# Keys and values of the memory tokens made feature-major, from memory given feature-major as well

## The chip, the cores and the metric

The kernel runs on one core of a Trainium2 chip. The metric is the device time of one launch in microseconds (us), lower is better. Three runs of the kernel before gave a median of 2762.11 us (2761.31 to 2764.7).

## The reference

One layer of a streaming encoder with 512 tokens of width 2048, in fp32: a token mixer of four parts, cross-attention of 4 heads into 256 memory tokens, and a SwiGLU network. Only the cross-attention touches the change:

```
def memory_cross_attention(h, m, wq, wkv, wo):      # m = rmsnorm(mem, g[MEM_NORM]), 256 x 2048
    q = (h @ wq).reshape(bsz, T, XA_HEADS, XA_HEAD_DIM)
    k, v = jnp.split(m @ wkv, 2, axis=-1)           # 4 heads of 512 columns each
    s = jnp.einsum('bthd,bmhd->bhtm', q, k) * XA_HEAD_DIM ** -0.5
    p = jax.nn.softmax(s, axis=-1)
    o = jnp.einsum('bhtm,bmhd->bthd', p, v).reshape(bsz, T, D_MODEL)
    return o @ wo
```

The norm of a memory token is one factor for its row (from the mean square of its 2048 values) and a gain per feature, which the kernel multiplies into the weights.

## The kernel before, in words

Every fp32 operand of a matrix product is split into a high and a low part (hi by a rounding copy on ScalarE, the engine ACT; lo by a subtraction on VectorE, the engine DVE). A product is three matmuls: hi by hi, hi by lo, lo by hi (`mul3`, L177 to L179). Weights arrive as `raw` tiles of 256 rows by 512 columns (512 KB, issued on the SyncE queue, SP), and L161 and L162 make `whi` and `wlo` of them, in two halves of 128 x 512, with the gain as a factor. Each of `raw`, `whi` and `wlo` has three buffers. PSUM has five accumulators `mm` and three tiles `ps` for transposes and small products.

The program begins with **the key stage**, from 0 to about 113 us. `k_proj` runs `kv_proj` for four heads. The memory (256 x 2048) is loaded with tokens on the partitions in eight pieces `memt`; 32 transposes on the matrix engine (L265) make it feature-major, and it is split into the tiles called `act`. For a head, `proj_b` makes eight chunks of 256 features: memory stationary, weights moving, for each of two token tiles and two feature tiles three matmuls of 512 columns. That is 96 matmuls a head, into two `mm` accumulators with tokens on the partitions. ACT evicts each with the token's factor `rmem` (L290), eight transposes (L293) make the head feature-major, the result is split into `kh` and `kl`, and both go to DRAM. `finish` computes `rmem` from the loaded rows, and the feature-major memory is written to DRAM (`m_d`) for later.

Then `x_startup` loads the 512 token rows as four tiles `xt` of 1 MB, normalises them and transposes them (L231, 64 transposes) for the first projection out of x (`z`). Its code stands behind the key stage, but the order of instructions on each engine is made by a scheduler over the whole program, so that loads and norms of x, and the first weights of z, stand among the last instructions of the key stage.

**The value stage** (about 715 to 832 us) reads `m_d` back (`v_load`) and runs the same `kv_proj` for four value heads, while the last mixer (`ssd`, marked as high priority) puts its own small products, and much DVE work, between them. Later `value_out` multiplies the values by the output weights `xa_wo`, evicts with an ACT copy, and writes `vw_d`.

## Time and profile before

| | before |
|---|---|
| median of three runs | 2762.11 us |
| the profiled execution | 2761.12 us |
| its span in the trace | 2759.1 us |
| around the span | 2.0 us |
| PE (matmuls) busy | 2673.8 us, 97% |
| DVE, ACT busy | 1942.6 us (70%), 1266.6 us (46%) |
| granted TensorE clock, mean | 0.99 |
| memory traffic | 428.08 MB, mean 155 GB/s |

PE does matmuls, PEld is its weight load, which overlaps. The span is the time from the first to the last recorded instruction. The page cuts the span in stretches and names, for each instruction, what ended the wait before it.

### The profile page before, as it was taken

Reading aid. Unit: us, or ns where it says so; the run is one execution under the profiler, and the core shown is the slowest. Engines: PE = TensorE matmul, PEld = TensorE weight load, DVE = VectorE, ACT = ScalarE, POOL = GpSimd, SP = SyncE. Lnnn points to the kernel's source line nnn. Section 1 sums busy time; section 2 is a strip of 40 time slices with the busy share of each in tenths; the row PEclk is TensorE's granted clock in tenths of the full one; section 3 lists DMA queues with packets and bytes.
Section 4 is the critical chain, followed back from the end, with each engine's and each line's share of the span. In section 5 each row is a group of like instructions: output and inputs, shape, how many; then the busy total and the mean of one; then the engine's idle time right before and its main releaser. Section 6 shows DMA issues by size and latency. Waiting matters only on the chain.

```text
span 2759.1 us, 35296 instructions
## 1 busy us (share of the span) xinstructions
PE 2673.8 (97%) x13426; PEld 2246.2 (81%) x13426; DVE 1942.6 (70%) x2866; ACT 1266.6 (46%) x1927; POOL 148.9 (5%) x225
## 2 busy tenths in 40 slices
PE   8999999999999999999978999999999998999997
PEld 6788788878788877888867888888888887888885
DVE  5735557446662255434589989898989898999985
ACT  5623423233552245423455454454445455655552
POOL 0000000100000001000000000000000000000004
PEclk9999999999999999999989999999999999999998
DMA  8632322343676358532553443333334336577765
GB/s 292 238 102 86 96 69 81 107 130 115 222 241 232 98 171 308 186 106 85 197 207 131 148 121 121 126 117 124 121 120 123 118 115 225 202 193 189 183 172 186
DMA packets 159283, 428.08 MB, mean 155 GB/s; under 512 B 18173, under 2 KB 30346, under 8 KB 148234
## 3 DMA queue, kind: packets, MB, share of 16 engines
q1 hardware_dynamic: 140682, 355.57, 39.7%
q0 software_dynamic: 18432, 70.27, 8.8%
q8 instruction: 105, 1.72, 0.3%
q14 instruction: 64, 0.52, 0.1%
HBM read 351.30 MB, written 74.47 MB: 154 GB/s over the span
## 4 chain that ended last, share of the span: by engine, by line
PE 83%; DVE 8%; DMA 5%; ACT 2%; issue 2%; SPq 0%; POOL 0%; DVEq 0%; ACTq 0%; POOLq 0%
PE mm L178 17%; PE mm L179 17%; PE mm L177 17%; PE mm L1088 11%; PE ps L1088 8%; PE mm L1091 6%; PE ps L1091 4%; DVE wlo L162 1%; DMA raw<-in_xa_wkv_dram 1%; DVE wlo L992 1%; PE ps L533 1%; PE ps L537 1%; DMA vw_d<-at_e 1%; DMA raw<-in_w_gu_dram 1%; DVE L L992 1%
## 5 line engine op out<-in xcount | busy, mean ns | idle before, releaser
L162 DVE SCALAR_TENSOR_TENSOR wlo<-raw,PA,whi 128x512 fp32r<-128x512 f32 x368 | 263.4, 748 | 300.4 <-ACT whi L161 300.0
L161 ACT ACTIVATE whi<-raw,PA 128x512 fp32r<-128x512 f32 x368 | 248.5, 720 | 399.5 <-PE mm L178 213.3
L1088 PE MATMUL mm<-L,whi 128*128 128x512 f32 x1448 | 367.7, 396 | 15.7 <-ACT f_x L1111 8.6
L177 PE MATMUL mm<-act,whi 128*128 128x512 f32 x832 | 330.3, 397 | 0.0
L179 PE MATMUL mm<-act,wlo 128*128 128x512 f32 x832 | 327.4, 394 | 0.0
L178 PE MATMUL mm<-act,whi 128*128 128x512 f32 x832 | 326.9, 393 | 0.0
L1088 PEld LDWEIGHTS mm<-L,whi 128*128 128x128 f32 x1448 | 263.5, 191 | 64.7 <-ACT f_x L1111 9.6
L991 ACT CAST whi<-raw 128x1024 fp32r<-128x1024 f32 x176 | 185.1, 1052 | 237.4 <-PE mm L1088 71.2
L1088 PE MATMUL ps<-L,whi 128*128 128x512 f32 x1016 | 254.8, 392 | 0.0
L177 PE MATMUL mm<-whi,act 128*128 128x512 f32 x640 | 251.9, 394 | 2.9 <-ACT act L158 2.5
L178 PE MATMUL mm<-wlo,act 128*128 128x512 f32 x640 | 251.1, 393 | 1.8 <-DVE wlo L162 1.8
L179 PE MATMUL mm<-whi,act 128*128 128x512 f32 x640 | 250.2, 392 | 0.2 <-DVE act L159 0.2
L159 DVE TENSOR_TENSOR wlo<-raw,whi 128x1024 fp32r<-128x1024 f32 x92 | 112.4, 1225 | 192.2 <-ACT whi L158 192.0
L177 PE MATMUL mm<-whB,B 128*128 128x512 f32 x592 | 231.1, 392 | 7.7 <-ACT whB L991 7.7
L178 PE MATMUL mm<-wlB,B 128*128 128x512 f32 x592 | 231.3, 391 | 1.3 <-DVE wlB L992 1.3
L179 PE MATMUL mm<-whB,B 128*128 128x512 f32 x592 | 231.0, 390 | 0.0
L992 DVE TENSOR_TENSOR wlo<-raw,whi 128x1024 fp32r<-128x1024 f32 x176 | 214.3, 1219 | 5.2 <-ACT whi L991 5.2
L1091 PEld LDWEIGHTS mm<-L,wlo 128*128 128x128 f32 x1448 | 198.0, 191 | 18.1 <-DVE wlo L992 4.0
L1088 PEld LDWEIGHTS ps<-L,whi 128*128 128x128 f32 x1016 | 182.7, 189 | 32.6
L1091 PE MATMUL mm<-L,wlo 128*128 128x256 f32 x1448 | 203.2, 283 | 2.8 <-DVE wlo L992 2.8
L991 ACT CAST whi<-sum 128x1024 fp32r<-128x1024 f32 x132 | 138.0, 1048 | 128.8 <-DVE wlo L992 64.6
L992 DVE TENSOR_TENSOR wlo<-sum,whi 128x1024 fp32r<-128x1024 f32 x132 | 161.7, 1225 | 43.3 <-ACT whi L991 42.5
(443 smaller groups left out, 4628.8 us busy)
## 6 DMA issues: line engine op xcount, KB each, us to landing
raw<-in_w_gu_dram SPq DMA_DIRECT2D x186, 512.0 KB, 3.5
raw<-in_w_in_dram SPq DMA_DIRECT2D x88, 512.0 KB, 3.7
rawB<-in_w_down_dram SPq DMA_DIRECT2D x40, 1024.0 KB, 5.5
raw<-in_xa_wkv_dram SPq DMA_DIRECT2D x64, 512.0 KB, 4.5
raw<-in_w_out_dram SPq DMA_DIRECT2D x32, 512.0 KB, 3.9
raw<-in_xa_wo_dram SPq DMA_DIRECT2D x32, 512.0 KB, 6.0
raw<-in_xa_wq_dram SPq DMA_DIRECT2D x32, 512.0 KB, 3.9
raw<-vw_d SPq DMA_DIRECT2D x28, 512.0 KB, 4.4
```

The source lines that it names most:

```text
L159: nc.vector.tensor_tensor(lo, src, hi.bitcast(F32), op=ALU.subtract)
L161: nc.scalar.activation(hi, src, AF.Copy, scale=scale)
L162: nc.vector.scalar_tensor_tensor(lo, src, scale, hi.bitcast(F32), op0=ALU.mult, op1=ALU.subtract)
L177: nc.tensor.matmul(o, ah, bh, start=start, stop=False, skip_group_check=reopen)
L178: nc.tensor.matmul(o, ah, bl, start=False, stop=False, skip_group_check=reopen)
L179: nc.tensor.matmul(o, al, bh, start=False, stop=stop, skip_group_check=reopen)
L533: nc.tensor.matmul(h64(tp)[:, h], A[:, h], Xe[:, h], start=True, stop=True)
L537: nc.tensor.matmul(h64(tp)[:, h], Pm[:, h], half(Y, s, 1)[:, h], start=True, stop=True)
L991: nc.scalar.copy(hl[0], src)
L992: nc.vector.tensor_tensor(hl[1], src, hl[0].bitcast(F32), op=ALU.subtract)
L1088: nc.tensor.matmul(bank, wh[:, k], t[k].rearrange("p s n -> p (s n)"), start=k == 0 and m in (1, 2, 5), stop=k == 7, **kw)
L1091: nc.tensor.matmul(bank[:, 0:256], wl[:, k], t[k][:, 0], start=False, stop=k == 7, **kw)
```

## The change

A second copy of the memory, transposed on the host, is an input: `mem_t`, four blocks of 128 features x 4 x 256 tokens. Each block is loaded (512 KB) and split with its high and low part side by side in one tile. In `kv_proj` the weights become the stationary operand and the memory the moving one: for each pair of feature tile and output tile one matmul of 512 columns (`wh` by hi and lo together) and one of 256 columns (`wl` by hi). The results are feature-major at once, in four `mm` accumulators a head; ACT copies the 256 columns that hold `wh` by lo out of PSUM, and DVE adds the other 256 to them. The 32 transposes of the memory and the eight of each head are gone.

The token factors now lie along the free axis. For the keys `rmem` is written to DRAM (`r_d`, 1 KB) and read back broadcast to all partitions as `R` (`k_r`), and DVE multiplies each key tile by it. The rows with tokens on the partitions are still loaded (`memr`, two tiles of 1 MB, in the chunks 5 and 7 of the first head) for the norm alone. For the values the factor moves to `value_out`, whose eviction becomes an ACT activation with a scale.

```
-    def mem_lhs(mt):
-        return lambda k, t: tuple(m[:, k % 8, t * P:(t + 1) * P] for m in mt[k // 8])
+    def mem_tiles():
+        return [ap_.tile([P, 4, 2, MEM], F32R, name="act") for _ in range(4)]
     def kv_proj(mt, c0, dst, pl, pre=None, done=None):
-        def evict(t, o):
-            kt = pl.tile([P, 512], F32, name="k_t", bufs=2)
-            nc.scalar.activation(kt, o, AF.Copy, scale=rmem[:, t:t + 1])
-            tp = ps.tile([P, 4, P], F32, name="ps")
+        o = [mm.tile([P, 512], F32, name="mm") for _ in range(4)]
+        for kc in range(KT // 2):
+            wh, wl = weights(xa_wkv, kc * 2 * P, c0, 4)
+            if pre:
+                pre(kc)
             for j in range(4):
-                nc.tensor.transpose(tp[:, j], kt[:, j * P:(j + 1) * P], ident)
-            split(hi[:, :, t * P:(t + 1) * P], lo[:, :, t * P:(t + 1) * P], tp)
-        proj_b(mem_lhs(mt), KT, xa_wkv, 0, c0, evict, range(MT_), 4, pre=pre, done=done)
+                js = slice(j * P, (j + 1) * P)
+                for k in (2 * kc, 2 * kc + 1):
+                    nc.tensor.matmul(o[j], wh[:, k % 2, js], mt[k // 4][:, k % 4].rearrange("p s m -> p (s m)"),
+                                     start=k == 0, stop=k == KT - 1, **kw)
+                for k in (2 * kc, 2 * kc + 1):
+                    nc.tensor.matmul(o[j][:, 0:MEM], wl[:, k % 2, js], mt[k // 4][:, k % 4, 0], start=False,
+                                     stop=k == KT - 1, **kw)
+        kt = []
+        for j in range(4):
+            kt.append(pl.tile([P, MEM], F32, name="k_t", bufs=4))
+            nc.scalar.copy(kt[j], o[j][:, MEM:])
+            nc.vector.tensor_tensor(kt[j], o[j][:, 0:MEM], kt[j], op=ALU.add)
+        R = done() if done else None
+        for j in range(4):
+            if R is not None:
+                nc.vector.tensor_tensor(kt[j], kt[j], R, op=ALU.mult)
+            split(hi[:, j], lo[:, j], kt[j])
...
+        def factors():
+            ss = sm.tile([P, MT_], F32, name="nr_s2")
+            for t in range(MT_):
+                sumsq(rows[t], ss[:, t:t + 1], pl)
+            mean_rsqrt(rmem, ss, MT_, D)
+            nc.sync.dma_start(r_d.rearrange("t p -> p t"), rmem)
+            nc.sync.dma_start(R, r_d.rearrange("t p -> (t p)").partition_broadcast(P))
+            for q in range(4):
+                nc.gpsimd.dma_start(m_d[q], mt[q].rearrange("p a s b -> p (a s b)").bitcast(F32))
+            return R
...
         for c in range(4):
             def evict(t, o):
                 e = pl.tile([P, 512], F32, name="at_e", bufs=2)
-                nc.scalar.copy(e, o)
+                nc.scalar.activation(e, o, AF.Copy, scale=rmem[:, t:t + 1])
```

The scheduler gives the engines new orders in the key stage, at the passage to z and in the value stage; elsewhere only the eviction of `value_out` has another operation. Three places follow. In a row stand the line, the operation, what it writes and what it reads; numbers tell buffers apart. Lines of the changed kernel are one higher in the helpers (`split` is L160 and L163 there) and eleven higher behind `k_proj`.

First, DVE at the passage from the first to the second key head. Before (`wlo_456` to `wlo_496` are the second head's weights, `kl_130` the first head's keys):

```order
L162 SCALAR_TENSOR_TENSOR wlo_456<-raw_453,PA_84,whi_455 128x512 x2
L159 TENSOR_TENSOR kl_130<-ps_401,kh_129 128x4x128
L139 COPY PB_85<-ps_425 128x93
L162 SCALAR_TENSOR_TENSOR wlo_476<-raw_473,PA_84,whi_475 128x512
L159 TENSOR_TENSOR kl_130<-ps_410,kh_129 128x4x128
L140 TENSOR_SCALAR PH_86<-PB_85 128x88
L162 SCALAR_TENSOR_TENSOR wlo_476<-raw_473,PA_84,whi_475 128x512
L162 SCALAR_TENSOR_TENSOR wlo_496<-raw_493,PA_84,whi_495 128x512 x2
```

After (`wlo_465` is the third weight tile of the second head, `k_r` is `R`):

```order
L163 SCALAR_TENSOR_TENSOR wlo_465<-raw_462,PA_84,whi_464 128x512
L286 TENSOR_TENSOR k_t_347<-k_t_347,k_r_128 128x256
L286 TENSOR_TENSOR k_t_350<-k_t_350,k_r_128 128x256
L286 TENSOR_TENSOR k_t_353<-k_t_353,k_r_128 128x256
L160 TENSOR_TENSOR kl_130<-k_t_347,kh_129 128x256
L160 TENSOR_TENSOR kl_130<-k_t_350,kh_129 128x256
L160 TENSOR_TENSOR kl_130<-k_t_353,kh_129 128x256
L286 TENSOR_TENSOR k_t_356<-k_t_356,k_r_128 128x256
L163 SCALAR_TENSOR_TENSOR wlo_465<-raw_462,PA_84,whi_464 128x512
L163 SCALAR_TENSOR_TENSOR wlo_489<-raw_486,PA_84,whi_488 128x512
```

The multiplications by `R` and three of the four low parts now stand between the two halves of one weight tile of the second head.

Second, DVE at the passage from the keys to z. Before (`wlo_1231`, `wlo_1263` and `wlo_1295` are the first weights of z, `act_1021` the transposed x):

```order
L318 TENSOR_SCALAR xt_1091<-xt_1091,nr_r_1096 128x2048
L162 SCALAR_TENSOR_TENSOR wlo_1231<-raw_1228,PA_84,whi_1230 128x512 x2
L162 SCALAR_TENSOR_TENSOR wlo_1263<-raw_1260,PA_84,whi_1262 128x512 x2
L159 TENSOR_TENSOR kl_798<-ps_963,kh_797 128x4x128
L162 SCALAR_TENSOR_TENSOR wlo_1295<-raw_1292,PA_84,whi_1294 128x512
L159 TENSOR_TENSOR kl_798<-ps_972,kh_797 128x4x128
L159 TENSOR_TENSOR act_1021<-ps_1112,act_1020 128x4x128
```

After (`wlo_1330` is the first weight tile of z, `kl_857` the last head's keys, the names with `1195` to `1198` the norm of the fourth x tile, whose load is the last of four). The five rows ahead of this piece are the scaling of the third x tile, the last two additions of the head and two of its low parts:

```order
L286 TENSOR_TENSOR k_t_1060<-k_t_1060,k_r_128 128x256
L286 TENSOR_TENSOR k_t_1063<-k_t_1063,k_r_128 128x256
L238 TENSOR_SCALAR mr_v_1196<-nr_s_1192 128x1
L160 TENSOR_TENSOR act_1120<-ps_1211,act_1119 128x4x128
L160 TENSOR_TENSOR kl_857<-k_t_1060,kh_856 128x256
L160 TENSOR_TENSOR kl_857<-k_t_1063,kh_856 128x256
L149 TENSOR_SCALAR nr_r_1195<-mr_v_1196 128x1
L160 TENSOR_TENSOR act_1120<-ps_1218,act_1119 128x4x128
L150 TENSOR_SCALAR nr_r_1195<-nr_r_1195 128x1
L160 TENSOR_TENSOR act_1120<-ps_1225,act_1119 128x4x128
L152 TENSOR_TENSOR rsq_t_1198<-nr_r_1195 128x1
L163 SCALAR_TENSOR_TENSOR wlo_1330<-raw_1327,PA_84,whi_1329 128x512
```

The first low weights of z stood ahead of the last keys and of the transposed x, and now stand behind both and behind the scaling of three x tiles. On the SP queue the loads of x at this passage stood so before (`raw` out of `xa_wkv` are weights of the keys, out of `w_in` those of z; the first x tile is four rows ahead of this piece):

```order
L316 DMA xt_1049<-in_x_dram 128x2048
L166 DMA raw_841<-in_xa_wkv_dram 128x2x512
L166 DMA raw_861<-in_xa_wkv_dram 128x2x512
L166 DMA raw_881<-in_xa_wkv_dram 128x2x512
L316 DMA xt_1070<-in_x_dram 128x2048
L316 DMA xt_1091<-in_x_dram 128x2048
L166 DMA raw_901<-in_xa_wkv_dram 128x2x512
L166 DMA raw_921<-in_xa_wkv_dram 128x2x512
L166 DMA raw_941<-in_xa_wkv_dram 128x2x512
```

And after, with all four x tiles:

```order
L327 DMA xt_1127<-in_x_dram 128x2048
L167 DMA raw_982<-in_xa_wkv_dram 128x2x512
L167 DMA raw_1006<-in_xa_wkv_dram 128x2x512
L167 DMA raw_1030<-in_xa_wkv_dram 128x2x512
L327 DMA xt_1148<-in_x_dram 128x2048
L327 DMA xt_1169<-in_x_dram 128x2048
L327 DMA xt_1190<-in_x_dram 128x2048
L167 DMA raw_1327<-in_w_in_dram 128x2x512
L167 DMA raw_1359<-in_w_in_dram 128x2x512
```

The last three weight tiles of the keys stood behind the x tiles; now three x tiles stand back to back behind these weights, straight ahead of z's.

Third, DVE at the passage from the first to the second value head. Before (`wlo_6312` is a weight tile, the names with `sd` belong to the mixer that runs between):

```order
L682 TENSOR_TENSOR sd_L_5919<-ps_5943,sd_L_5919 128x512
L162 SCALAR_TENSOR_TENSOR act_5735<-ps_5906,PB_85,act_5734 128x128
L682 TENSOR_TENSOR sd_L_5919<-ps_5943,sd_L_5919 128x512
L162 SCALAR_TENSOR_TENSOR wlo_6312<-raw_6309,PA_84,whi_6311 128x512
L695 TENSOR_TENSOR sd_t_5966<-ps_5963,sa_eG_1676 128x512
L688 TENSOR_TENSOR sd_y_5961<-ps_5952,sd_Xd_5939 128x512
L709 TENSOR_TENSOR sd_h_5972<-ps_5969,sd_h_5972 128x512
L697 TENSOR_TENSOR sd_y_5961<-sd_y_5961,sd_t_5966 128x512
L162 SCALAR_TENSOR_TENSOR wlo_6312<-raw_6309,PA_84,whi_6311 128x512
```

After (`wlo_6453` is the second weight tile of the second value head, `kl_6201` the first head's values; its fourth addition and first low part stand just ahead of this piece):

```order
L160 TENSOR_TENSOR kl_6201<-k_t_6401,kh_6200 128x256
L708 TENSOR_TENSOR sd_y_6060<-sd_y_6060,sd_t_6065 128x512
L720 TENSOR_TENSOR sd_h_6071<-ps_6068,sd_h_6071 128x512
L725 TENSOR_TENSOR sd_y_6060<-sd_y_6060,sd_z_6074 128x512
L669 TENSOR_TENSOR sd_L_6112<-sd_L_6112,C_83 128x1024
L733 TENSOR_SCALAR sd_vv_6082<-sd_ss_6077 128x2
L160 TENSOR_TENSOR kl_6201<-k_t_6404,kh_6200 128x256
L149 TENSOR_SCALAR sd_rr_6084<-sd_vv_6082 128x2
L160 TENSOR_TENSOR kl_6201<-k_t_6407,kh_6200 128x256
L150 TENSOR_SCALAR sd_rr_6084<-sd_rr_6084 128x2
L163 SCALAR_TENSOR_TENSOR wlo_6453<-raw_6450,PA_84,whi_6452 128x512
```

The evictions of the value heads stood far behind this piece before; the last addition and the four low parts of the first head now stand ahead of the second half of `wlo_6453`.

59 lines of the change are left out of this document (22 added, 37 removed).

## The prediction

> **What bounds the kernel now.** I read the page's first part, its chain that ended last, and then the two stretches that the change rewrites.
>
> ```profile
> PE 2673.8 (97%) x13426; PEld 2246.2 (81%) x13426; DVE 1942.6 (70%) x2866; ACT 1266.6 (46%) x1927; POOL 148.9 (5%) x225
> PE 83%; DVE 8%; DMA 5%; ACT 2%; issue 2%; SPq 0%; POOL 0%; DVEq 0%; ACTq 0%; POOLq 0%
> ```
>
> PE bounds it nearly everywhere, so a matmul removed counts in full, and so does each microsecond in which PE waits. The idle time sits in few places. The windows of the key stage, of the passage to z and of the first value heads (columns: PE, PEld, DVE, ACT, POOL busy, granted clock, DMA share, GB/s):
>
> ```profile
> 30.00:40.00 10.00, 7.79 (x38) 5.77 (x36) 5.98 (x17) 4.87 (x8) 1.07 (x2) 1.00 0.84 301
> 40.00:50.00 10.00, 10.00 (x48) 8.19 (x47) 5.72 (x10) 5.05 (x9) 1.07 (x2) 1.00 1.03 334
> 80.00:90.00 10.00, 8.79 (x43) 6.99 (x42) 7.85 (x27) 7.35 (x12) 0.00 (x0) 1.00 0.92 325
> 100.00:110.00 10.00, 9.25 (x40) 7.07 (x39) 9.13 (x21) 6.54 (x12) 0.00 (x0) 1.00 0.64 203
> 110.00:120.00 10.00, 9.11 (x60) 7.09 (x60) 8.74 (x15) 8.32 (x16) 1.07 (x2) 1.00 0.80 258
> 720.00:780.00 60.00, 55.98 (x289) 46.26 (x288) 52.96 (x125) 33.85 (x79) 0.00 (x0) 1.00 0.60 200
> ```
>
> PE loses 2.2 us in 30 to 40, 1.2 in 80 to 90, 0.75 and 0.89 around the passage to z. The DMA engines are at 0.84 to 1.03 in the key stage, and DVE is at 53 of 60 us among the value heads: the two resources that the change loads more.
>
> **Fewer transposes.** PE's timeline, around four memory transposes:
>
> ```profile
> 30.34 0.39 PE L179 MATMUL mm<-whi,act 128*128 128x512 f32 x1
> 30.57 0.60 PE L265 MATMUL ps<-C,memt 128*128 128x128 f32 x4
> 30.92 0.48 PE L177 MATMUL mm<-whi,act 128*128 128x512 f32 x1
> 31.23 0.40 PE L178 MATMUL mm<-wlo,act 128*128 128x512 f32 x1
> ...
> 32.16 0.40 PE L179 MATMUL mm<-whi,act 128*128 128x512 f32 x1
> 34.59 0.50 PE L177 MATMUL mm<-whi,act 128*128 128x512 f32 x1 [2.03 <-ACT act L158]
> ```
>
> The plain pace of the key heads is in PE's rows of the last head, five steps in 1.13 us, 0.226 each:
>
> ```profile
> 109.16 0.39 PE L177 MATMUL mm<-whi,act 128*128 128x512 f32 x1
> ...
> 110.29 0.39 PE L179 MATMUL mm<-whi,act 128*128 128x512 f32 x1
> ```
>
> Start to start, L179 to L178 is 0.89 us with four transposes between, of which the two matmuls take 0.23 each: 0.44 for four, 0.11 each. 32 of memory, 32 of keys and 32 of values go: 96 x 0.11 = **-10.7 us**.
>
> **Another mix of matmuls.** A head had 96 of 512 columns; it gets 64 of 512 and 64 of 256, two and two. Such pairs run elsewhere in this kernel:
>
> ```profile
> 1996.94 1.11 PE L1091 MATMUL mm<-L,wlo 128*128 128x256 f32 x8
> 1997.89 2.00 PE L1088 MATMUL ps<-L,whi 128*128 128x512 f32 x8
> 1999.73 1.12 PE L1091 MATMUL ps<-L,wlo 128*128 128x256 f32 x8
> ```
>
> Eight narrow ones take 0.95 us to the next start, 0.119 each; eight wide ones 1.84, 0.230. A head becomes 64 x (0.230 + 0.119) = 22.3 us against 96 x 0.226 to 0.228 = 21.8. Eight heads: **+4.4 us** (3.5 to 5).
>
> ```profile
> L1091 PEld LDWEIGHTS mm<-L,wlo 128*128 128x128 f32 x1448 | 198.0, 191 | 18.1 <-DVE wlo L992 4.0
> ```
>
> In that pattern a weight load lasts 191 ns while the narrow matmul's spacing is 119: loads overlap matmuls and each other. The Trainium skill ("TensorE: Matmul & The Clock Gate", Part 3, "The mechanism") says that a load overlaps matmuls in flight only when its row group differs; by that rule the 256 additional loads would lie bare. It is a rival below.
>
> **The start.** ACT and PE timelines:
>
> ```profile
> 7.65 1.34 ACT L161 ACTIVATE whi<-raw,PA 128x512 fp32r<-128x512 f32 x2
> 9.70 0.79 PE L177 MATMUL mm<-whi,act 128*128 128x512 f32 x1
> ```
>
> Before, the first matmul follows the weights and one transposed 512-wide split. Now ACT must round a 128x1024 block and DVE subtract one, 1.05 and 1.22 us by L991 and L992 of these shapes:
>
> ```profile
> L991 ACT CAST whi<-raw 128x1024 fp32r<-128x1024 f32 x176 | 185.1, 1052 | 237.4 <-PE mm L1088 71.2
> L992 DVE TENSOR_TENSOR wlo<-raw,whi 128x1024 fp32r<-128x1024 f32 x176 | 214.3, 1219 | 5.2 <-ACT whi L991 5.2
> ```
>
> PE's first matmul waits for both, since its moving operand holds the low part too. ACT ends at 9.0 + 1.1 = 10.1, DVE at 11.3: **+1.6 us** (1 to 3).
>
> **The passage to the second key head.** Durations of the key stage, grouped by shape:
>
> ```profile
> L162 DVE SCALAR_TENSOR_TENSOR wlo<-raw,PA,whi 128x512 fp32r<-128x512 f32 x72 | 50.9, 748 | 21.4 <-ACT whi L161 21.2
> L159 DVE TENSOR_TENSOR act<-ps,act 128x512 fp32r<-128x512 f32 x24 | 15.9, 688 | 2.2 <-ACT act L158 2.0
> L242 ACT ACTIVATE junk<-xt 128x2048 bf16<-128x2048 f32 x4 | 7.7, 1912 | 4.5 <-DMA xt<-in_x_dram 4.5
> L151 DVE TENSOR_TENSOR rsq_t<-nr_r 128x1 f32<-128x1 f32 x18 | 2.8, 158 | 0.4
> L290 ACT ACTIVATE k_t<-mm,rmem 128x512 f32<-128x512 f32 x8 | 5.3, 681 | 1.4 <-PE mm L179 1.3
> L318 DVE TENSOR_SCALAR xt<-xt,nr_r 128x2048 f32<-128x2048 f32 x4 | 5.1, 1287 | 0.1
> L352 DVE TENSOR_TENSOR gw<-gw,PA 128x256 f32<-128x256 f32 x1 | 0.4, 427 | 0.8 <-DMA gw<-in_w_in_dram 0.8
> ```
>
> L352 is the one 128x256 operation: I take 0.43 for each new narrow DVE one. Let E be the end of the first head. On ACT the four copies out of PSUM now stand ahead of the second head's first `whi`; some 0.4 us each (half of L290's 0.68 and a fixed part) and behind the last matmul, they make PE wait **+1.2 us** (0 to 2).
>
> Then `R`. `rmem` is done at about E-1, since its last steps stand on DVE between the additions. The write of `r_d` and the broadcast read follow each other on SP. Their nearest relatives by the DMA issues (KB each, us to landing):
>
> ```profile
> raw<-in_xa_wkv_dram SPq DMA_DIRECT2D x32, 512.0 KB, 5.3
> gw<-in_w_in_dram SPq DMA_DIRECT2D x32, 4.0 KB, 4.2
> ga_row<-in_gdn_dt_bias_dram SPq DMA_DIRECT2D x1, 2.0 KB, 5.6
> ```
>
> Two legs of 4.2 to 5.6 put `R` at E+7.4 to E+10.2. By the first place of the order, four products and three low parts (7 x 0.43 = 3.0) then precede the second half of `wlo_465` (0.75): E+11 to E+14. PE holds, until it needs that half, two chunks of 2.8 us and 2.0 of a third, from E+1.2 on: to E+8.8. It waits 2.4 to 5.2, I take **+3.4** (0 if both legs take under 3 us; 6 if the rows of memory come late). Behind `R`'s read on SP stands a weight load (`raw_486`): issued at about E+4 and landed 5.3 later, it is no later than that half. The page of the Trainium skill on DMA ("DMA: Bandwidth & Descriptors", "Anatomy of one DMA") gives a fixed cost of about 2.0 us for a transfer; two of them would put `R` at E+3 and leave no wait.
>
> **Waits that go.** The 2.2 us in 30 to 40 end with a split of the transposed memory (the row at 34.59), the 1.2 in 80 to 90 with the eviction ahead of the key transposes:
>
> ```profile
> 86.09 0.39 PE L179 MATMUL mm<-whi,act 128*128 128x512 f32 x1
> 87.69 1.24 PE L293 MATMUL ps<-C,k_t 128*128 128x128 f32 x8 [1.21 <-ACT k_t L290]
> ```
>
> Both waits' instructions are gone: **-3.4 us** (-3.4 to 0, since the weights behind the first came late as well).
>
> **The passage to z.** Before, on ACT, SP and PE:
>
> ```profile
> 93.53 1.91 ACT L242 ACTIVATE junk<-xt 128x2048 bf16<-128x2048 f32 x1 [1.84 <-DMA xt<-in_x_dram]
> 97.65 0.37 SPq L166 DMA_DIRECT2D raw<-in_xa_wkv_dram  x1
> 110.97 1.23 PE L293 MATMUL ps<-C,k_t 128*128 128x128 f32 x8 [0.29 <-ACT k_t L290]
> 112.04 0.60 PE L231 MATMUL ps<-C,xt 128*128 128x128 f32 x4
> ```
>
> The last matmul of the keys starts at 110.3, the last key weights were issued at 97.7, and x's second square, which waits for its data, already starts at 93.5. Now three x tiles are issued behind the last key weights, some 12 us ahead of the keys' end (call it Z). With those weights they are 3.7 MB, at 300 to 334 GB/s 11 to 12 us: the last lands at about Z. ACT's squares of the second and third (2 x 1.9) stand ahead of the key evictions and end at about Z-1. From there DVE has, by the second place of the order: the norm chain (eleven small operations of 0.16 with gaps, 2.1), two additions and two products (1.7), the scaling (1.3), two additions, two low parts and two products (2.6), then three transposed pieces of x (2.1), two low parts (0.9) and the first half of z's `wlo` (0.75), in all 11: it is ready at about Z+9 to Z+10. Meanwhile PE has three sets of transposes and three matmuls, 2.0 us. It waits 7.6, and 0.7 for the fourth x tile: 8.3 against 0.75 + 0.89 before, **+6.7 us** (1 to 9; 1 if x lands 5 us earlier and DVE's chain fits before Z).
>
> **More data.** The memory is now read twice: 2 MB, at some 334 GB/s 6 us of DMA time, in a stretch at 0.84 to 1.03; and the writes of `m_d` start early. Weights prefetched three deep hide most, I take **+1.5** (0 to 6).
>
> **The value stage.** A head trades two low parts of 0.69 for four additions and four low parts of 0.43: +2.1 us on a DVE with 7 free in 60. By the third place of the order, two narrow operations more stand ahead of a weight half that PE waits for, at three passages: 3 x 0.86 = **+2.6** (0 to 6, all additional work of three heads). The scale in `value_out` replaces a copy on ACT by an activation like L290 (0.68), on an engine that is at 46% and evicts while PE runs the next product: nothing; if each of the 32 became 0.1 longer and all lay bare, 3 us.
>
> **Sum.** -10.7 + 4.4 + 1.6 + 1.2 + 3.4 - 3.4 + 6.7 + 1.5 + 2.6 = +7.3 on the profiled 2761.1 us (span 2759.1 and 2.0 around it): 2768.4. The median lies 1.0 higher: **2769 us**.
>
> **Rivals.**
>
> 1. The saving shows. If x lands early enough that DVE has z's first weights at Z+2, and `R` comes back within 3 us a leg, the passages cost 1 and 0 and the value stage 0: -10.7 + 4.4 + 1.6 - 3.4 + 1 = -7, 2755 us. For it: PE is at 97% and waits little in all. Against: z's weights have moved behind the keys on DVE. It decides from about 6 us less waiting at the two passages; half of it gives 2762.
> 2. The DMA engines bind in the first head: the 2 MB cost their 6 us, and `memr` and so `R` come 3 later: +7.3 + 4.5 + 3 = 2777 us. For it: shares of 1.03. Against: 258 GB/s in 110 to 120, so there are pauses.
> 3. Weight loads stand bare: 256 x 0.191 = 49 us, 2818 us. This is that page's rule; the pair row at 0.119 speaks against it.
>
> **Chances.** The forecast 0.50, rival 1 whole or in part 0.29 (0.13 of it below 2756.6), rival 2 0.16, rival 3 0.01, others 0.04. The range is 2756 to 2779; the forecast's own 2764 to 2774. A measurement tells 0.2%, 5.5 us, from no change: same is 2756.6 to 2767.6. Faster 0.15, same 0.33 (most of rival 1's rest and the forecast's low end), slower 0.52.
>
> **What would show it.** PE without L265 and L293, some 22.3 us a head; a PE wait for `wlo` some 9 us into the second key head, ended behind `k_r`; the longest wait, 5 to 9 us, at the passage to z, behind DVE's low parts. PE waits under 3 us there and a later pace as before would prove it wrong, as would narrow matmuls spaced over 0.13 us.

## The result, and the profile after

| | before | after |
|---|---|---|
| median | 2762.89 us (4 runs) | 2788.38 us (4 runs, 2785.26 to 2790.43) |
| ratio | | 1.0095, 95% interval 1.0083 to 1.0107 |
| profiled execution | 2761.12 us | 2785.26 us |
| its span | 2759.1 us | 2783.3 us |
| granted clock, mean | 0.990 | 0.985 |

The change costs 25.5 us by the medians and 24.1 us between the two profiled executions. The prediction had the side right (slower) and the size wrong: 2769 us with a range to 2779.

The first line of the page after reads:

```profile
PE 2676.7 (96%) x13586; PEld 2257.1 (81%) x13586; DVE 1955.6 (70%) x2912; ACT 1268.6 (46%) x1955; POOL 148.6 (5%) x225
```

PE is busy only 2.9 us longer than before (2676.7 against 2673.8), although the execution is 24.1 us longer. So the time went into idle PE, and a mean over the whole kernel does not say where. A look at the same instruction in both traces does. I take two: the transposes of `gd_q` in the mixer that follows z, and the attention's transposes of `at_p` after the value stage. Grouped by source line, with instructions, min/median/max ns, first and last start, before:

```profile
L439 PE MATMUL ps<-C,gd_q x16: 270/272/327, 310.8 to 315.6; 128*128 128x128 f32 x16
L877 PE MATMUL ps<-C,at_p x32: 270/272/329, 1136.2 to 1312.4; 128*128 128x128 f32 x32
```

and after:

```profile
L450 PE MATMUL ps<-C,gd_q x16: 270/272/328, 328.8 to 333.6; 128*128 128x128 f32 x16
L885 PE MATMUL ps<-C,at_p x32: 270/272/330, 1155.4 to 1331.5; 128*128 128x128 f32 x32
```

The first has moved by 18.0 us, the second by 19.1 to 19.2. The key stage and the passage to z therefore cost 18.0, the value stage 1.1 to 1.2, and 5.0 of the 24.1 come later. The position of `gd_q` is the measure for most of the experiments, since it leaves out all that is later.

**Three places in the first 140 us.** The windows after, with the columns of those before (PE, PEld, DVE, ACT, POOL busy, granted clock, DMA share, GB/s):

```profile
20.00:30.00 10.00, 9.68 (x56) 8.27 (x54) 3.67 (x5) 4.68 (x6) 0.53 (x1) 1.00 1.03 423
30.00:40.00 10.00, 5.11 (x20) 4.40 (x21) 5.10 (x12) 5.72 (x7) 0.53 (x1) 0.83 1.02 382
50.00:60.00 10.00, 4.64 (x15) 3.47 (x16) 4.60 (x11) 4.73 (x10) 0.49 (x1) 0.66 0.45 138
120.00:130.00 10.00, 4.45 (x24) 3.31 (x23) 9.42 (x34) 7.55 (x17) 0.00 (x0) 0.85 0.35 120
130.00:140.00 10.00, 8.51 (x26) 6.33 (x25) 7.73 (x22) 3.13 (x7) 1.05 (x2) 0.64 0.76 258
```

PE loses about 5 us in 30 to 40, 5 in 50 to 60 and 7 between 120 and 140. In all these windows but the first the granted clock, the share of its full speed that PE got, is below 1.00 as well. PE's timeline after (start, duration, instruction, and in brackets the wait before it and who ended it):

```profile
11.29 1.22 PE L273 MATMUL mm<-act,whi 128*128 128x512 f32 x2 [7.18 <-DVE act L160]
16.28 0.63 PE L273 MATMUL mm<-act,whi 128*128 128x512 f32 x2
16.74 0.40 PE L276 MATMUL mm<-act,wlo 128*128 128x256 f32 x2
16.97 0.63 PE L273 MATMUL mm<-act,whi 128*128 128x512 f32 x2
34.89 1.22 PE L273 MATMUL mm<-act,whi 128*128 128x512 f32 x2 [5.22 <-DVE act L160]
43.35 1.21 PE L273 MATMUL mm<-act,whi 128*128 128x512 f32 x4 [1.00 <-ACT whi L162]
55.21 1.41 PE L273 MATMUL mm<-act,whi 128*128 128x512 f32 x2 [6.00 <-ACT whi L162]
126.93 1.09 PE L232 MATMUL ps<-C,xt 128*128 128x128 f32 x4 [3.92 <-DVE xt L329]
129.31 1.65 PE L178 MATMUL mm<-whi,act 128*128 128x512 f32 x3 [1.29 <-ACT whi L162]
132.45 0.80 PE L179 MATMUL mm<-wlo,act 128*128 128x512 f32 x1 [1.49 <-DVE wlo L163]
133.89 1.06 PE L179 MATMUL mm<-wlo,act 128*128 128x512 f32 x2
134.75 1.06 PE L180 MATMUL mm<-whi,act 128*128 128x512 f32 x2
```

The reader is to see three things.

- At 16.28 two wide matmuls take 0.46 us to the next start and two narrow ones 0.23: 0.23 and 0.115 each.
- There are two long waits in the key heads, at 34.89 behind the split of a memory block (5.22), and at 55.21 behind `whi` (6.00). The passage to z has three waits in a row (3.92, 1.29, 1.49).
- At 133.89 two wide matmuls take 0.86 us to the next start, 0.43 each instead of 0.23. This is the half clock, and it stands behind the waits.

In the wait before 55.21 the granted clock is 0.98 from 50 to 52 and 0.50 in the two microseconds after that, while PE starts nothing:

```profile
52.00:54.00 2.00, 0.00 (x0) 0.00 (x0) 0.00 (x0) 0.00 (x0) 0.00 (x0) 0.50 0.35 82
```

So here the clock is low before the first slow matmul; late operands of the matmuls behind the wait are not the reason.

**The ledger**, up to an instruction among z's products (the first transpose of `gf`, at 176.13 us before and at 196.09 after), is +19.96:

| term | us |
|---|---|
| first matmul, 9.70 to 11.29 | +1.6 |
| idle between PE's rows, 5.3 to 20.5 | +15.2 |
| 64 transposes at 0.11 | -7.0 |
| other mix, four heads of 32 x 0.69 = 22.2 against 21.8 | +1.6 |
| half clock: half of 3.5 us behind 34.8, of 3.5 behind 55.2, of some 6.6 in 127 to 137 | +6.8 |
| not assigned | +1.8 |

Between there and `gd_q`, 2.0 us come back. The kernel before has a stretch at low clock there, and the changed one has not (before in the first fence, after in the second):

```profile
186.00:196.00 10.00, 10.00 (x40) 8.14 (x40) 3.22 (x13) 3.96 (x13) 0.00 (x0) 0.83 0.36 116
```

```profile
206.00:216.00 10.00, 10.00 (x45) 8.24 (x45) 3.29 (x13) 4.55 (x14) 0.00 (x0) 1.00 0.39 119
```

A mean of 0.83 over ten us is 3.4 us at half clock, or 1.7 us lost.

**What ends the long waits.** SP's, ACT's and DVE's timelines after:

```profile
18.17 0.56 SPq L299 DMA_DIRECT2D memt<-in_mem_t_dram  x1
32.54 1.04 ACT L159 CAST act<-memt 128x1024 fp32r<-128x1024 f32 x1 [1.10 <-DMA memt<-in_mem_t_dram]
42.02 0.37 SPq L311 DMA_DIRECT2D r_d<-rmem  x1
42.48 0.42 SPq L167 DMA_DIRECT2D raw<-in_xa_wkv_dram  x1
51.15 0.34 SPq L312 DMA_DIRECT2D k_r<-r_d  x1
54.43 1.33 ACT L162 ACTIVATE whi<-raw,PA 128x512 fp32r<-128x512 f32 x2 [9.30 <-DMA raw<-in_xa_wkv_dram]
56.15 1.10 DVE L286 TENSOR_TENSOR k_t<-k_t,k_r 128x256 f32<-128x256 f32 x3 [0.21 <-DMA k_r<-r_d]
```

The first two lines are the wait at 34.89. The fourth memory block is issued at 18.17 and can be cast only at 32.54, 14.4 us later, in windows at a share of 1.03 and 1.02. The others are the wait at 55.21. The write of `r_d` is issued at 42.02, and the read behind it only at 51.15, when the write is done: 9.1 us for 1 KB. The weight load issued in between, at 42.48, is landed at 54.4, 12 us later, while the window 50 to 60 has a DMA share of 0.45. ACT's `whi` waits for that load for 9.30 us. PE waited for this `whi` of the third weight tile, not for the low part that stands behind the multiplications by `R`. But `R` is late as well: its products start at 56.15, and the second half of the third tile's low part stands behind them on DVE and starts at 58.50. PE takes it at 59.30. By this order `R` would have held PE about as long had the load been in time. Both come from the same write.

In the DMA records of the trace, 272 packets of four bytes start between 42.5 and 43.5 and last 9 ns at most. The 2 KB packets of the weights behind them last up to 3146 ns, where 84 ns is usual.

### The profile page after: what moved, and what is told of

It reads as the page before. It is cut to its first block, busy times and chain, and to the rows that moved or that the text cites. A ratio compares the mean times of both kernels' runs of the same rounds, so it can differ in the third digit from the quotient of the medians.

```text
span 2783.3 us, 35687 instructions
## 1 busy us (share of the span) xinstructions
PE 2676.7 (96%) x13586; PEld 2257.1 (81%) x13586; DVE 1955.6 (70%) x2912; ACT 1268.6 (46%) x1955; POOL 148.6 (5%) x225
## 5 line engine op out<-in xcount | busy, mean ns | idle before, releaser
L163 DVE SCALAR_TENSOR_TENSOR wlo<-raw,PA,whi 128x512 fp32r<-128x512 f32 x368 | 262.4, 746 | 314.1 <-ACT whi L162 312.0
L178 PE MATMUL mm<-act,whi 128*128 128x512 f32 x832 | 329.8, 396 | 0.0
L179 PE MATMUL mm<-act,whi 128*128 128x512 f32 x832 | 326.1, 392 | 0.0
L160 DVE TENSOR_TENSOR wlo<-raw,whi 128x1024 fp32r<-128x1024 f32 x92 | 112.3, 1224 | 188.3 <-ACT whi L159 188.0
L273 PE MATMUL mm<-act,whi 128*128 128x512 f32 x512 | 167.8, 408 | 21.1 <-DVE act L160 12.4
L180 PEld LDWEIGHTS mm<-act,wlo 128*128 128x128 f32 x832 | 156.3, 188 | 32.3 <-issue 0.5
L179 PEld LDWEIGHTS mm<-act,whi 128*128 128x128 f32 x832 | 156.4, 188 | 30.9 <-issue 0.7
```

The costliest lines, as they stand in the source:

```text
L160: nc.vector.tensor_tensor(lo, src, hi.bitcast(F32), op=ALU.subtract)
L163: nc.vector.scalar_tensor_tensor(lo, src, scale, hi.bitcast(F32), op0=ALU.mult, op1=ALU.subtract)
L178: nc.tensor.matmul(o, ah, bh, start=start, stop=False, skip_group_check=reopen)
L179: nc.tensor.matmul(o, ah, bl, start=False, stop=False, skip_group_check=reopen)
L180: nc.tensor.matmul(o, al, bh, start=False, stop=stop, skip_group_check=reopen)
L273: nc.tensor.matmul(o[j], wh[:, k % 2, js], mt[k // 4][:, k % 4].rearrange("p s m -> p (s m)"), start=k == 0, stop=k == KT - 1, **kw)
```

## The experiments

What was to be told apart:

- In the second key head: the **pieces** of the `r_d` write (256 of four bytes) hold up what is queued behind them, or the **order** on SP and the round trip of `R` do.
- In the first head: the **bytes** in the stretch, of which the early write-back of `m_d` is a part, or the **order** in which block and rows are asked for.
- At the passage to z: the **late loads of x**, or DVE's greater work.
- The half clock: a consequence of the waits, or something by itself.
- The value stage: a small price, or none.

Three kernels undo one suspected cost each, one puts a suspect into the kernel before, and further ones add up, reorder and bring back. The two single traces differ by chance as well, so the kernel before was run once more as a control. Its `gd_q` is at 311.7 and its `at_p` at 1138.0:

```profile
L439 PE MATMUL ps<-C,gd_q x16: 270/272/328, 311.7 to 316.5; 128*128 128x128 f32 x16
L877 PE MATMUL ps<-C,at_p x32: 270/273/329, 1138.0 to 1314.2; 128*128 128x128 f32 x32
```

So differences under 1 us at `gd_q`, and under 2 us at `at_p`, between two traces say nothing. In the table each ratio is to the runs of the kernel before that were taken along with that kernel; `gd_q` is from one trace each.

| kernel | median us | ratio to before [95%] | `gd_q` at us |
|---|---|---|---|
| before | 2762.89 | 1 | 310.8 (control 311.7) |
| after | 2788.38 | 1.0095 [1.0083, 1.0107] | 328.8 |
| tiny_write | 2764.15 | 1.0009 [1.0000, 1.0019] | 312.4 |
| row_write | 2779.73 | 1.0060 [1.0045, 1.0075] | 321.4 |
| no_writeback | 2780.93 | 1.0066 [1.0051, 1.0081] | 322.9 |
| x_early | 2779.52 | 1.0059 [1.0044, 1.0074] | 318.8 |
| three_repairs | 2762.44 | 1.0000 [0.9991, 1.0010] | 307.2 |
| on_chip_factors | 2759.98 | 0.9988 [0.9978, 0.9997] | 306.7 |
| values_only | 2763.74 | 1.0005 [0.9996, 1.0014] | 310.6 |
| rows_later | 2788.87 | 1.0095 [1.0074, 1.0115] | 330.2 |
| row_plus_tiny | 2786.61 | 1.0083 [1.0066, 1.0100] | 327.0 |
| keep_warm | 2782.93 | 1.0068 [1.0053, 1.0083] | 327.7 |
| control (before again, one run) | 2765.2 | | 311.7 |

**tiny_write.** The kernel before, with the write of `r_d` alone added; nothing reads it.

```
             mean_rsqrt(rmem, ss, MT_, D)
+            nc.sync.dma_start(r_d.rearrange("t p -> p t"), rmem)
```

> The kernel before with one transfer added on SP: the factors of the memory tokens written to DRAM in 256 pieces of 4 bytes, as the changed kernel does, read by nobody. Theory A (the small pieces hold up the DMA engines): the weight load issued behind the write lands 9 us or more after its issue, against 3.9 in the kernel before; PE gets a wait of 2 to 7 us in the second key head, where it had none, and the time rises by 3 to 9 us, to 2766 to 2772. Rival B (the write is harmless; the changed kernel waits for the chain write, read, multiply): the load lands in 4 to 6 us and the time stays within 3 us of 2763.

It costs 0.1%, with an interval that reaches down to no change, and `gd_q` moves by 1.6 us against the first trace of before, by 0.7 against the control. ACT's and PE's timelines:

```profile
51.11 1.34 ACT L162 ACTIVATE whi<-raw,PA 128x512 fp32r<-128x512 f32 x2 [5.28 <-DMA raw<-in_xa_wkv_dram]
56.62 0.51 PE L178 MATMUL mm<-whi,act 128*128 128x512 f32 x1 [1.15 <-ACT whi L162]
```

The write was issued at 37.71 and the weight load behind it at 39.41. ACT waited for that load and took it at 51.11, 11.7 us after its issue, so theory A has its late load. But this was a tile that PE needed later than the corresponding one after the change, and PE waited only 0.29 us for it. Its new wait of 1.15 us is for the next tile, which SP issued only at 51.07. The forecast wait of 2 to 7 us and the 3 to 9 us in time did not come. Taken alone this run is inconclusive: a late load is there, its price is small.

**row_write.** The changed kernel, but the factors are transposed on PE first, so that `r_d` is written as two pieces of 512 bytes.

```
-            nc.sync.dma_start(r_d.rearrange("t p -> p t"), rmem)
+            tp = ps.tile([P, P], F32, name="ps")
+            nc.tensor.transpose(tp[0:MT_], rmem, ident)
+            rr = pl.tile([P, P], F32, name="k_rr")
+            nc.vector.tensor_copy(rr[0:MT_], tp[0:MT_])
+            nc.sync.dma_start(r_d, rr[0:MT_])
```

> The changed kernel, with the factors transposed on PE to two rows first, so that the write to DRAM is two pieces of 512 bytes instead of 256 of 4; the broadcast read stays. Theory A: the write lands in 3 to 5 us instead of 9.1, the weight loads near it in 4 to 6 us instead of 12, and of the wait in the second key head (6.2 us, and 1.8 at the half clock behind it) 1 to 4 us are left: 2780 to 2785 in all. Rival B (two transfers one after the other are the wait, whatever their pieces): the wait stays over 5 us, 2786 to 2790.

`gd_q` comes 7.4 us earlier. SP's timeline with the write, a weight load and the read behind it, ACT's use of that load, and the one wait that PE has left there:

```profile
42.68 0.26 SPq L315 DMA_DIRECT2D r_d<-k_rr  x1
44.85 0.37 SPq L167 DMA_DIRECT2D raw<-in_xa_wkv_dram  x1
45.32 0.58 SPq L316 DMA_DIRECT2D k_r<-r_d  x1
48.76 1.34 ACT L162 ACTIVATE whi<-raw,PA 128x512 fp32r<-128x512 f32 x2 [2.43 <-DMA raw<-in_xa_wkv_dram]
53.44 0.39 PE L276 MATMUL mm<-act,wlo 128*128 128x256 f32 x1 [0.79 <-DVE wlo L163]
```

The write is done within 2.6 us instead of 9.1, and the wait of 6.00 is gone. The Trainium skill ("DMA: Bandwidth & Descriptors", "Specifications") gives 512 bytes as the least size of a transfer at full rate, and a read, modification and write for anything smaller. The two writes agree with it in kind (2.6 us at most against 9.1). In this kernel the order on SP is another one as well: the third weight tile stands ahead of the write. The load that stands behind it (44.85) is taken at 48.76, 3.9 us after its issue, although a load of `gw` in 128 packets of 32 bytes was issued in between (42.99). So not every write, and not every transfer in small pieces, delays a load behind it. row_plus_tiny puts the four-byte pieces back.

**row_plus_tiny.** row_write, and in addition a write in four-byte pieces that nothing reads, ahead of the third weight tile. `R` is read from the write in two pieces.

```
             nc.sync.dma_start(r_d, rr[0:MT_])
+            nc.sync.dma_start(r_x.rearrange("t p -> p t"), rmem)
```

> The kernel with the factors written in two pieces of 512 bytes, and beside it a write of the same factors in 256 pieces of 4 bytes that nobody reads; it stands on SP ahead of the third weight tile of the second head, where the changed kernel has its own. Theory A (the small pieces themselves): the weight tile behind it lands 9 us or more after its issue, the wait of about 6 us in the second head is back, and the time with it, 2785 to 2789. Rival (the other order of loads on SP gave the gain of the row write): it stays within 2 us of that kernel, 2778 to 2782.

Of the 7.4 us, 5.6 are back (327.0 against 321.4). SP's, ACT's and PE's timelines:

```profile
42.29 0.37 SPq L317 DMA_DIRECT2D r_x<-rmem  x1
43.32 2.19 SPq L168 DMA_DIRECT2D raw<-in_xa_wkv_dram  x2
54.77 2.69 ACT L163 ACTIVATE whi<-raw,PA 128x512 fp32r<-128x512 f32 x4 [9.38 <-DMA raw<-in_xa_wkv_dram]
55.55 1.41 PE L274 MATMUL mm<-act,whi 128*128 128x512 f32 x2 [6.07 <-ACT whi L163]
```

The wait of 6 us and ACT's wait of 9.4 are the same as after the change, although nothing waits for this write. The load landed 11.4 us after its issue, against 3.9 in row_write. `R` is not early here: its read is issued at 49.58, 6.6 us behind its write (42.98) instead of 2.6, so the small pieces hold up that write too. But here DVE makes both halves of the third tile's low part (from 55.53) ahead of the multiplications by `R` (56.86), so neither `R`'s round trip nor the order of DVE can make this wait. This shows it: the write in small pieces delays the weight load that is issued behind it. In all seven kernels that have this write, that load is taken 11.0 to 13.1 us after its issue.

**no_writeback.** `m_d` is not written in the key stage. The value stage loads `mem_t` and splits it again.

```
-            for q in range(4):
-                nc.gpsimd.dma_start(m_d[q], mt[q].rearrange("p a s b -> p (a s b)").bitcast(F32))
...
-            nc.sync.dma_start(mt[q].rearrange("p a s b -> p (a s b)").bitcast(F32), m_d[q])
+            raw = pl.tile([P, 4, MEM], F32, name="memt", bufs=2)
+            nc.sync.dma_start(raw, mem_t[q])
+            split(mt[q][:, :, 0], mt[q][:, :, 1], raw)
```

> The changed kernel without the 4 MB written to DRAM in the key stage; the value stage loads the transposed memory (2 MB instead of 4) and splits it again, four copies on ACT and four subtractions on DVE more. Theory C (these writes, now early, crowd the DMA engines in the first head): the fourth memory block lands in 5 to 8 us instead of 14, the wait of 5.4 us near 30 and the 1.7 at the half clock behind it go, and the key stage ends 5 to 8 us earlier; the value stage costs 0 to 4 more; 2780 to 2786. Rival D (the 2 MB of memory rows, issued ahead of the fourth block, are the cause): the fourth block still lands in 10 us or more, PE still waits over 3 us, 2786 to 2792.

`gd_q` comes 5.9 us earlier, and the value stage costs the same 1.2 us. SP's, ACT's and PE's timelines:

```profile
18.69 0.46 SPq L299 DMA_DIRECT2D memt<-in_mem_t_dram  x1
26.02 1.04 ACT L159 CAST act<-memt 128x1024 fp32r<-128x1024 f32 x1
47.78 1.41 PE L273 MATMUL mm<-act,whi 128*128 128x512 f32 x2 [5.05 <-ACT whi L162]
```

The fourth block is cast 7.3 us after its issue instead of 14.4, and the wait at 34.89 is gone. The memory's rows land 8.4 us after their issue instead of 13.8. The other wait stays (5.05 at 47.78, with 1.41 more for a low part behind it), only earlier: it does not need the first one. The rows were still loaded here, and no run takes them alone away.

**rows_later.** The changed kernel, with the rows of the memory asked for behind the fourth block instead of ahead of it; no byte less.

```
-            elif kc >= 5:
+            if kc >= 6:
```

> The changed kernel with the fourth memory block issued ahead of both tiles of memory rows. Theory C (the write-back crowds the engines): the block still lands in 9 us or more and PE waits 3 us or more near 30. Rival D (the rows ahead of it in the queue): it lands in under 8 us, the wait falls under 2, and the factors come about as late as before or up to 3 us later, so that 2 to 5 us of the 7.1 are gained.

Nothing is gained (330.2 against 328.8; two runs, one trace). The fourth block is cast at 25.27, 10.2 us after its issue instead of 14.4, and its wait is gone, but PE waits for weights instead:

```profile
36.37 1.41 PE L273 MATMUL mm<-act,whi 128*128 128x512 f32 x2 [2.14 <-ACT whi L162]
57.80 1.41 PE L273 MATMUL mm<-act,whi 128*128 128x512 f32 x2 [7.36 <-ACT whi L162]
```

The wait in the first head is 2.14 instead of 5.22, and yet the head ends only 0.9 us earlier (PE's row of L139 behind it starts at 41.16 instead of 42.10); the second head loses more than that. Neither expectation came out in full. With no_writeback beside it, the bytes decide in the first head. At 382 to 423 GB/s this other order only chose which load was late.

**x_early.** The loads and norms of x are written ahead of the last key head in the program.

```
             else:
+                if h == 3:
+                    xs = x_load(pl)
                 kv_proj(mt, h * XHD, k_d[h], pl, done=lambda: R)
```

> The changed kernel with the loads and norms of x written in the program ahead of the last key head, so that the x tiles are issued during the second and third heads. Theory E (x comes too late, which holds ACT and DVE at the passage to z): the waits at the passage, 8.2 us and 3.3 at the half clock, fall under 4 together, 2778 to 2783. Rival F (the evictions of the last key head on DVE, ahead of z's first weights, hold PE even when x is there): PE still waits over 5 us at the passage, 2785 to 2789. If the x tiles crowd the second head instead, its wait grows by what the passage gains.

`gd_q` comes 10.0 us earlier, the most of the three. The windows of the passage:

```profile
120.00:130.00 10.00, 9.75 (x60) 7.68 (x58) 8.76 (x20) 8.94 (x20) 1.06 (x2) 1.00 0.60 220
130.00:140.00 10.00, 10.00 (x62) 8.39 (x61) 9.66 (x16) 6.84 (x15) 0.00 (x0) 1.00 0.45 143
```

The four loads of x by their source line (last two numbers: first and last start), here and after the change:

```profile
L330 SPq DMA_DIRECT2D xt<-in_x_dram x4: 458/462/591, 42.4 to 74.3; - x4
```

```profile
L327 SPq DMA_DIRECT2D xt<-in_x_dram x4: 430/474/908, 99.4 to 108.2; - x4
```

With the loads 34 to 57 us earlier PE has no wait over 0.3 us at the passage, and the clock stays at 1.00. The additions, products and low parts of the last key head still stand among z's first low weights on DVE (121.5 to 127.5), so they were not the cause, and rival F falls. The norms of x and some of its transposes moved along with the loads, and this run does not part them. The gain of 10.0 is about the idle time there (0.33 + 3.92 + 1.29 + 1.49 = 7.0) and the half clock behind it (3.3).

**three_repairs.** row_write, no_writeback and x_early together.

> The three changes of the runs before in one kernel: factors written in two pieces of 512 bytes, no write-back of the memory (the value stage splits it again), x loaded ahead of the last key head. If the three causes are separate, their gains in the key stage add up (7.5, 6.0 and 10.0 us against the 18.0 that the changed kernel had lost by 311 us): 5 us ahead of the kernel before at that point, about 4 ahead behind the value stage, and 2757 to 2763 in all. If they are one crowding of the DMA engines, or one wait only uncovers the next, PE keeps more than 5 us of waits between the first head and z, and the time is 2764 to 2772.

2762.44 us, no different from before (1.0000, 0.9991 to 1.0010). At `gd_q` the three add up to 21.5 us (328.8 to 307.2), where the sum of the single gains is 23.3. So the three account for all of the 18.0 us lost and 3.5 more, where 5 was expected. Behind the value stage the lead is 1.7 us, and in the median nothing is left of it. Two windows:

```profile
30.00:40.00 10.00, 9.20 (x54) 7.82 (x53) 6.77 (x24) 6.49 (x12) 0.00 (x0) 1.00 0.61 202
50.00:60.00 10.00, 9.52 (x52) 7.68 (x51) 6.91 (x22) 5.85 (x8) 0.00 (x0) 1.00 1.00 375
```

PE is at 9.2 and 9.5 where it was at 5.11 and 4.64, and the clock is at 1.00 with no change made for it.

**on_chip_factors.** The version to which the three point. The norm comes from the squares of the feature-major memory, summed by small products; the factors are spread to all partitions by a product of ones with a diagonal; the rows of the memory, `r_d` and `m_d` are no longer needed; x is loaded early.

```
+                sq = pl.tile([P, 4, MEM], F32, name="memq", bufs=1)
+                nc.scalar.activation(sq, raw, AF.Square)
+                nc.vector.tensor_reduce(m, sq.rearrange("p a m -> p m a"), axis=AX.X, op=ALU.add)
...
+                for q in range(4):
+                    nc.tensor.matmul(ss[:, t:t + 1], red[q][:, t * P:(t + 1) * P], ones[:, 0:1], start=q == 0, stop=q == 3)
...
+                nc.vector.tensor_scalar(dg, ident, rmem[:, t:t + 1], None, op0=ALU.mult)
+                nc.tensor.matmul(bp[:, t * P:(t + 1) * P], ones, dg, start=True, stop=True)
+            nc.vector.tensor_copy(R, bp)
```

> As the last, but the factors are made without any DMA: squares of the transposed memory blocks on ACT, their sums over the four features of a row on DVE, sums over the partitions by eight matmuls of one column, the root, and R by two matmuls of a matrix of ones with a diagonal of the factors. The memory rows (2 MB) and both transfers of the factors are gone. Waits for data that remain in the first and second head (the first by the last memory block, the second by R) should fall under 2 us together, and it should be 1 to 4 us below the kernel with the three repairs: 2753 to 2761, faster than the kernel before. If DVE, which now sums in the first head and then serves R behind the norm of an x tile, becomes late, PE gets a wait of 2 to 5 us in the second head, and it is no faster than that kernel.

2759.98 us: faster than before by 0.12% (0.9978 to 0.9997), 3.1 us, and the best of all, by an interval that only just leaves out no change. Two waits of 1.0 (at 42.34) and 1.8 us (at 63.87) are the long ones left in its key heads, both behind DVE; under 2 together was expected.

**values_only.** The kernel before, with the new value stage and `value_out` alone; the keys as before, and `m_d` read into tiles with high and low part side by side.

```
-                    kv_proj(mt, D + h * XHD, v_d[h], pl)
+                    kv_new(mt, D + h * XHD, v_d[h], pl)
...
-                nc.scalar.copy(e, o)
+                nc.scalar.activation(e, o, AF.Copy, scale=rmem[:, t:t + 1])
```

> The kernel before with the value stage alone made feature-major (its memory read from the old layout into the new), and the scale in the values' output. By the prediction's sum: 32 transposes fewer -3.5, other matmuls +2.2, evictions ahead of a weight half +2.6, in all +1.3: 2761 to 2766. If the passages cost nothing, -1.3 to -2: 2759 to 2762. If the kernel loses in the value stage what the trace of the changed kernel shows (1.1 us between 669 and 1136), the same is to be seen here.

1.0005 (0.9996 to 1.0014), and `at_p` at 1136.3 against 1136.2. The value stage and the new eviction of `value_out` neither cost nor gain anything that can be told.

**keep_warm.** The changed kernel with 24 matmuls that nothing reads, ahead of the matmul that waits in the second head. They were to keep the clock up and leave the wait.

```
+            if c0 == XHD and kc == 2:
+                w_ = ps.tile([P, 512], F32, name="ps")
+                for i in range(24):
+                    nc.tensor.matmul(w_, last[:, 0, 0:P], mt[0][:, 0].rearrange("p s m -> p (s m)"), start=i == 0, stop=i == 23)
```

> The changed kernel with 24 matmuls of 512 columns, whose result nobody reads, ahead of the matmul in the second head that waits 6.0 us for its weights. Theory (a long wait lowers the clock, and the matmuls behind it run at half pace for some 3.4 us): the matmuls behind the wait are spaced 0.23 us instead of 0.43 and the granted clock there is 1.00, the part of 1.8 us is gained, 2785 to 2788. Rival (the slow matmuls behind the wait have another reason, such as late operands): spacing and time as in the changed kernel, or later by what the additional matmuls overhang.

As a test of the clock it failed. The additional matmuls ran from 51.4 to 57, but the load came later still, and two waits were left with 1.6 us of work between them:

```profile
58.77 1.41 PE L279 MATMUL mm<-act,whi 128*128 128x512 f32 x2 [1.72 <-ACT whi L162]
62.56 0.58 PE L282 MATMUL mm<-act,wlo 128*128 128x256 f32 x1 [2.17 <-DVE wlo L163]
```

The window from 60 to 62 has a granted clock of 0.50 too. The median is 5.5 us lower than after, and this is not explained: in its trace `gd_q` is only 1.1 us earlier. The scheduler also placed the loads of x otherwise (94.4 to 113.9), and the waits at the passage to z are 1.82, 0.85 and 0.22 us, with the clock at 1.00 from 130 to 140. It is no measurement of the clock's price.

**control** is the kernel before, unchanged.

> The kernel before once more, for a second trace of it: how far two executions of one kernel lie apart at the passage to the last network (1411 to 1536 us), where every changed kernel lost 0.7 to 5 us against the first trace although its instructions there stand in the same order. If that is chance, this trace lies 1 to 4 us behind the first one there too; if the changed value stage causes it, it lies within 1 us of it.

Beside the two positions above, it shows a loss that comes and goes by chance. The passage to the last network begins with a wait of 2.0 us in both traces, and then runs at different clocks (the kernel before first, the control second):

```profile
1390.00:1395.00 5.00, 5.00 (x39) 4.53 (x40) 4.52 (x9) 4.99 (x7) 0.00 (x0) 1.00 0.26 94
```

```profile
1391.50:1396.50 5.00, 4.93 (x27) 4.38 (x27) 3.60 (x6) 4.56 (x7) 0.00 (x0) 0.66 0.30 98
```

From the transposes there to the first product of the network it is 21.8 us in the first and 23.5 in the control, with the same code. After the change it is 23.5 too. So 1.7 of the 5.0 us behind the value stage need no cause in the change. The other 3.3 are not settled. From `at_p` to the end the traces of the kernels with the changed value stage lose between 2.5 and 7.1 us against the first trace of before (after 5.0, values_only 2.8), the control loses 2.3 and tiny_write 0.6, and the order of the instructions there is the same.

## Why the prediction was right or wrong

**Fewer transposes, the other mix, the start: right.** Narrow matmuls are spaced 0.115 us (0.119 forecast), wide ones 0.23, and the first matmul starts 1.59 us later (1.6). The 256 additional weight loads cost nothing that the spacing shows, so rival 3 falls, and with it, for this kernel, the rule that it was taken from: a wide and a narrow matmul with loads of all 128 rows follow each other at 0.23 and 0.115, where a load in the open would add 0.19.

**The passage to the second key head, copies: right.** +1.2 was forecast; the wait at 43.35 is 1.00 us, and 1.2 by the spacing.

**The round trip of `R`: the step that failed in its mechanism.** The prediction took the write as a leg of 4.2 to 5.6 us, by rows of transfers that are large or come in larger pieces, and put the wait on the low part of a weight behind the multiplications. The write took 9.1 us, and `R` came late (DVE's multiplications at 56.15, the end E of the first head at 42.1, so E+14, against E+7.4 to E+10.2 forecast); the other figure that stood there, 2.0 us a transfer, would have put it at E+3. But `R` was not what ended PE's wait. The prediction let write and read follow each other on SP and asked only about the weight load behind the read (`raw_486`, the fourth tile). The third tile, `raw_462`, it took as landed, without a reason. In the trace that load stands between write and read, and it landed after 12 us: this is the wait. 3.4 was forecast. The wait measured 6.0, and with the half clock behind it the term is 7.8; taking the small pieces away, which cures both the load and `R`, gave 7.4.

**More data: mis-sized.** +1.5 was forecast, with rival 2 for more. The term was a wait of 5.2 and 1.8 of half clock behind it, in windows at 1.02 to 1.03, and no_writeback brought 5.9. The prediction had the share of 0.84 to 1.03 in sight and put 2 MB of reads on it; of the writes of `m_d` it said that they "start early" and gave them no price. They are the part whose removal ends the wait: four of 1 MB, issued at 11.6, 15.3, 21.2 and 35.1 us, the first three of them ahead of the wait. Rival 2, at a chance of 0.16, had the right limit at this place, the DMA engines, but put it on the 2 MB of reads.

**Waits that go: right, but others came.** -3.4 was forecast, and the waits of 2.0 and 1.2 are gone. New ones of 5.2, 1.0 and 6.0 took their place; they are counted in the other terms.

**The passage to z: right in its cause and nearly in the size of its wait, but not in its price.** Waits of 7.0 in the brackets against 8.3 forecast; x_early shows that the late x was the cause. The form was another: not one wait of 7.6 for DVE's low parts, but 3.92 for the scaling of x, 1.29 for ACT's `whi` and 1.49 for `wlo`, and the longest wait of all was the 6.00 in the second head, not one at this passage. (The parts of DVE's work that the prediction lists add up to 11.4 us, not 11, which makes its wait some 0.9 longer than the 7.6.) And the sum held the waits alone. The clock behind them was a half until 137, which is 3.3 us more.

**The half clock: missing from the sum.** At three places it makes 6.8 us, more than a third of the 18.0. The windows of before have 1.00 in the key stage, and so the prediction had no row for it there; the low clock behind a wait could have been seen later in the same trace (0.71 in 1400 to 1405, behind a wait of 4.04). The wait of 5.2, the 6.0, and the 3.9, 1.3 and 1.5 in a row, are each followed by matmuls at half pace; the wait of 1.0 at 43.35 is not. The Trainium skill ("TensorE: Matmul & The Clock Gate", "HAM oscillation") asks for no gap of PE over about 3.4 us, because the clock falls to a half. The rows of after agree with it (waits of 5.22, 6.00 and 3.92, then 0.43 us a wide matmul). keep_warm and the control add that shorter waits can do it as well: 1.7 and 2.2 with 1.6 of work between, and one of 2.0 in one execution of the same kernel and not in another. No run takes the clock's fall away and leaves the wait, so that the waits cause it is supported by where it stands, by its fall inside the wait before 55.21 and by its going with the waits in three_repairs, and not by an experiment of its own.

**The value stage: mis-sized to the safe side.** Saved transposes of 3.5, a mix of 2.2 and +2.6 for DVE make +1.3 by the prediction's terms. 1.1 was measured after, 1.2 in no_writeback and about 0 in values_only, all within what two traces of one kernel differ by. Most of the 1.1 does not lie among the value heads: the first product of `value_out` starts 18.1 us later than before (1021.5 against 1003.4), so up to there 0.1 is lost. In `value_out` the eviction takes 690 ns instead of 589, the 0.1 that the prediction thought possible, but the control loses 1.3 us in the same stretch with the old eviction.

**The sum.** To `gd_q` the terms gave about +6: -7.0 for the transposes, +2.2 for the mix, and all the others but the value stage (1.6 + 1.2 + 3.4 - 3.4 + 6.7 + 1.5 = 11.0). 18.0 were measured. The difference of 12 is the load behind the small write (+2.6 as a wait), the bytes of the first head (+3.7 as a wait) and the half clock (+6.8); the rest makes about -1. That the time came out above the whole range is thus three terms: one with the wrong mechanism, one too small, one left out. Behind the value stage 5.0 more came, of which 1.7 come and go by chance. Rival 1 fell with its condition: at the two passages PE waited more, not less. on_chip_factors shows how much saving there is with all three places mended: 3.1 us.

## What to carry to other kernels

A write to DRAM in four-byte pieces had two prices here, its own time and that of the transfers issued behind it on the same queue; the second stopped PE, and a transpose of the 256 numbers, or keeping them on the chip, took both away. Where the DMA engines are already at a share near 1, count every byte that a change moves into that stretch, the write-backs too; here another order only chose who waited. Price a wait of some microseconds on PE at its length and the half clock that may follow it, and look where the scheduler puts the loads of the next stage when a change shortens the code ahead of them.
